# Scores of 96 attention heads: pairs of heads in one 8 MB store, with two output buffers

## The chip, the core and the metric

The kernel runs on one core of a Trainium2 chip. The metric is the time of one execution on the device, in microseconds (us). Before the change it is 1062.99 us, the median of three runs (1062.89 to 1064.05).

The engines that matter here: TensorE (PE in the profile) multiplies, its weight loads have a row of their own (PEld), VectorE (DVE) and ScalarE (ACT) copy results from PSUM, TensorE's output memory, to SBUF, the working memory of 128 partitions. GpSimd (POOL) casts the inputs. SyncE (SP) issues the stores; sixteen DMA engines carry all transfers.

## What is computed

For every one of 8 x 12 = 96 heads, a matrix of 1024 x 1024 dot products of length 64:

```
q, k: float32 [8, 12, 1024, 64]
out = np.einsum('bhid,bhjd->bhij', q, k).astype(np.float32)
```

The inputs are 50 MB, the output is 403 MB: 4 MB for each head.

## The kernel before

The heads are taken in blocks of 2, 2, 4, 8, 8 and then six times 12 (`sizes`, line 33). Each block has its q and k as raw float32 (`load`, line 66), casts them to half precision on POOL (`cast_quads`, line 113, or `cast_rows`, line 90, for the first two blocks) and transposes them so that the 64 elements of a row lie along partitions: the first two blocks by TensorE (`transpose_rows`, line 147), the others by DVE (`transpose_quads`, line 139). The transposed `qT` and `kT` hold half of a block's heads in partitions 0 to 63 and the other half in partitions 64 to 127.

`scores` (line 156) then makes one head. Its 1024 output rows are split over 128 partitions, eight neighbouring rows to each. For each of these eight (index t) two products, of 512 columns each, use 128 columns of qT as weights and fill 1024 columns of a PSUM tile. From the second head on, a PSUM tile holds two t (`w = 2`: 128 x 2048, two such tiles in PSUM), and ACT copies each to the output tile `o_sb` (line 181); the first head uses smaller tiles, copied by DVE and ACT in turn (lines 179 and 181). When the head's tile is full, SP issues one store of 4 MB, in which each partition has 32 KB in one piece (line 185).

Program order is pinned on each engine. The order is written by hand: while a block is being computed, the casts of the next ones are queued on POOL (`to_half`, line 225), the transposes of the next block on DVE (the `side` work of `block`, line 238), and the loads of the block after that on ACT's queue (`LOADS`, line 263). A load waits until the casts have read the raw tile that it overwrites; a transpose waits for its cast.

The buffers: three output tiles of 32 KB a partition (`out_pool`, line 45), one of which first holds the raw inputs of the first three blocks (`early`, line 196); two raw tiles, five half precision tiles, and two each of qT and kT.

Of the kernel before, what the change touches and what calls it, by code (L numbers as in the profile page):

```python
# [9 lines left out]
F32 = mybir.dt.float32  # L10
P = 128

@with_exitstack
def kernel(
# [6 lines left out]
    nc = tc.nc  # L21

    B, H, S, D = q.shape
    NT = S // P
    BH = B * H
# [4 lines left out]
    kf = k.rearrange("b h s d -> (b h s) d")  # L30
    of = out.rearrange("b h i j -> (b h) i j")

    sizes = [2, 2, 4, 8, 8] + [12] * ((BH - 24) // 12)
    assert sum(sizes) == BH
    PE_BLOCKS = 2
    NMAX = max(sizes)
    CHUNK = 48 * 32

    consts = ctx.enter_context(tc.tile_pool(name="consts", bufs=1))
    ident = consts.tile([P, P], F16)  # L40

    in_pool = ctx.enter_context(tc.tile_pool(name="in_pool", bufs=2))
    half_pool = ctx.enter_context(tc.tile_pool(name="half_pool", bufs=5))
    tr_pool = ctx.enter_context(tc.tile_pool(name="tr_pool", bufs=2))
    out_pool = ctx.enter_context(tc.tile_pool(name="out_pool", bufs=3))

    pin = tc.keep_in_program_order

    def half_tile():
        half_sb = half_pool.tile([P, CHUNK], F16, tag="half")  # L50
        return half_sb

    class Block:
# [3 lines left out]
        def __init__(self, first, N, by_pe):  # L57
# [5 lines left out]
            self.halves = {}  # L63
            self.cut = max(1, self.R * 32 // CHUNK + (self.R * 32 % CHUNK > 0))

# [78 lines left out]
            )[:, c * m : (c + 1) * m]  # L144
            pin(nc.vector.transpose(out=dst, in_=src))  # L145

        def transpose_rows(self, x, ps_pool, copy):
            ps = ps_pool.tile([P, S], F32, tag="po")
            t_ps = ps.bitcast(F16)[:, : NT * P].rearrange("c (t m) -> c t m", m=P)
            for t in range(NT):  # L150
                pin(nc.tensor.transpose(t_ps[:, t], self.rows[x][:, t], ident))  # L151
            dst = (self.qT, self.kT)[x][:, :S].rearrange("c (m t) -> c m t", t=NT)
            src = t_ps.rearrange("c t m -> c m t")
            pin(copy(out=dst, in_=src))  # L154

        def scores(self, n, side, ps_pool, w):

            half, g = divmod(n, self.N // 2)
            cs = slice(half * D, (half + 1) * D)

            qT = self.qT.rearrange("c (g m t) -> c g t m", t=NT, m=P)
            kT = self.kT.rearrange("c (g j) -> c g j", j=S)
            o_sb = out_pool.tile([P, NT, S], F32, tag="out")
            for u in range(NT // w):
                ps = ps_pool.tile([P, w * S], F32, tag="po")
                for tt in range(w):
                    for j in range(2):
                        js = slice(j * 512, (j + 1) * 512)
                        at = tt * S + j * 512
                        pin(  # L170
                            nc.tensor.matmul(  # L171
                                ps[:, at : at + 512],
                                qT[cs, g, w * u + tt],
                                kT[cs, g, js],
                            )
                        )
                dst = o_sb[:, w * u : w * u + w].rearrange("p t j -> p (t j)")
                if w == 1 and u % 2:
                    pin(nc.vector.tensor_copy(out=dst, in_=ps))  # L179
                else:  # L180
                    pin(nc.scalar.copy(out=dst, in_=ps))  # L181
                for do in side.get(u, []):
                    do()
            pin(
                nc.sync.dma_start(
                    out=of[self.first + n].rearrange("(p t) j -> p (t j)", p=P),
                    in_=o_sb.rearrange("p t j -> p (t j)"),
                )
            )

    blocks, first = [], 0
    for i, N in enumerate(sizes):
        blocks.append(Block(first, N, i < PE_BLOCKS))
        first += N

    early = out_pool.tile([P, NT, S], F32, tag="out")
    raw = early.rearrange("p t j -> p (t j)")
    at = 0
    for b in blocks[:3]:
        for x in range(2):  # L200
# [11 lines left out]
    def next_load(eng):  # L212
        if stream:
            b, x = stream.pop(0)
            b.load(x, eng)
# [9 lines left out]
    def to_half(last):  # L225
        while casts:
            i, c = casts[0]
            if i > last or (blocks[i], c[0]) in stream:
                return
            blocks[i].cast_quads(*c)  # L230
            casts.pop(0)
# [3 lines left out]
            b.cast_rows(x)  # L235
    to_half(2)

    def block(i, heads, ps_pool, w):
        b = blocks[i]
        nxt = blocks[i + 1] if i + 1 < len(blocks) else None  # L240
        for n in heads:
            side = {}
            if nxt and nxt.by_pe:
                if n == 1:
                    side = {
                        u: [
                            lambda x=u // 2: nxt.transpose_rows(
                                x, ps_pool, nc.vector.tensor_copy
                            )
                        ]  # L250
                        for u in (1, 3)
                    }
            elif nxt:
                parts = nxt.chunks()
                some = [s for m, s in enumerate(parts) if m * b.N // len(parts) == n]
                side = {0: [lambda s=s: nxt.transpose_quads(*s) for s in some]}

            if n in LOADS.get(i, (6, 8)):
                side[1] = side.get(1, []) + [lambda: next_load(nc.scalar)]
            b.scores(n, side, ps_pool, w)  # L260
            to_half(i + 2 + (n == b.N - 1))

    LOADS = {0: (), 1: (), 2: (1, 3), 3: (4, 6), 4: (4, 6)}

    blocks[0].alloc()
    blocks[1].alloc()
    with tc.tile_pool(name="first_pool", bufs=4, space=bass.MemoryType.PSUM) as pool:
        for x in range(2):
            blocks[0].transpose_rows(x, pool, (nc.vector.tensor_copy, nc.scalar.copy)[x])
        block(0, [0], pool, 1)  # L270
    po_pool = ctx.enter_context(
        tc.tile_pool(name="po_pool", bufs=2, space=bass.MemoryType.PSUM)
    )
    block(0, [1], po_pool, 2)
    for i in range(1, len(blocks)):
        if i + 1 < len(blocks):
            blocks[i + 1].alloc()
        block(i, range(blocks[i].N), po_pool, 2)


# [28 lines left out]
```

## Time and profile before

| What | Value |
|---|---|
| Median of three runs | 1062.99 us |
| Profiled execution | 1063.03 us |
| its span, first to last instruction | 1061.2 us |
| HBM read / written | 50.33 MB / 402.65 MB, 427 GB/s over the span |
| TensorE products, line 171 | 1536 of 64 x 512, 696.9 us busy, 617 ns each |
| ACT copies, line 181 | 380 of 128 x 2048 at 1869 ns, 4 of 128 x 1024 at 1012 ns |
| DVE copies, line 179 | 4 of 128 x 1024 at 1224 ns |
| DVE transposes, line 145 | 48 of 128 x 1536, about 8.1 us; 20 of 128 x 1024, about 4.95 us |
| POOL casts, line 127 | 192 of 32 x 1536 at 1460 ns; 80 of 32 x 1024 at 1034 ns |
| Stores, line 185 | 96 of 4096 KB, 21.8 us from issue to landing (median) |

A row of the profile's groups gives line, engine, operation, the tiles written and read, count, time busy and mean duration of one. The products are pipelined, so that 617 ns is the length of one and not the distance between two. The slices cut the span into 40 equal parts; a digit is the share in tenths that an engine, or the mean of the 16 DMA engines, was busy. A wait is told as who waited, for what, how long in total, how often, and the longest. In the timeline a row merges neighbouring instructions of one kind; the bracket is the idle time before the first and what ended it.

### The profile page before, as it was taken

To read this page: it belongs to the slowest core of one execution; us is meant where nothing else is said; L and a number is where in the kernel's file an instruction comes from. 1 tells how busy PE (TensorE), PEld (TensorE's weight loads), DVE (VectorE), ACT (ScalarE), POOL (GpSimd) and SP (SyncE) were. 2 spreads that over 40 slices of the span, in tenths; PEclk is the share of its full clock that TensorE was granted. 3 is DMA by queue.
4 is the path that set the end of the run, shared out by engine and by line. 5 is a ranking of instruction groups with operands and counts; after the bars stand their busy time and mean duration, and the time that the engine had idled before them with its cause. 6 is when DMAs were issued, how large, how long until landed. Compare 5 with 4: busy or idle time off the path is not lost.

```text
span 1061.2 us, 4282 instructions
## 1 busy us (share of the span) xinstructions
PE 701.0 (66%) x1568; PEld 241.5 (23%) x1568; DVE 471.3 (44%) x75; ACT 697.3 (66%) x386; POOL 368.3 (35%) x286
## 2 busy tenths in 40 slices
PE   6866755765677557775577855777557777778770
PEld 2322211221222112221122211222112222222220
DVE  2999502990795007960079600795007950000000
ACT  4866755755677556775577755777557777777771
POOL 6967228607720463304633046320463200000000
DMA  9999999999999999999999999999999999999997
GB/s 375 434 435 434 434 432 429 432 430 429 429 434 431 429 438 429 435 422 428 434 434 433 425 424 437 432 431 426 432 430 434 434 434 430 430 435 430 433 431 319
DMA packets 17588, 453.25 MB, mean 427 GB/s; under 512 B 1952, under 2 KB 1952, under 8 KB 2976
## 3 DMA queue, kind: packets, MB, share of 16 engines
q1 hardware_dynamic: 14688, 406.85, 89.2%
q10 hardware_dynamic: 2880, 46.14, 10.3%
q8 instruction: 12, 0.20, 0.1%
q14 instruction: 8, 0.07, 0.0%
HBM read 50.33 MB, written 402.65 MB: 427 GB/s over the span
## 4 chain that ended last, share of the span: by engine, by line
DMA 71%; ACT 18%; PE 8%; issue 1%; DVE 0%; POOL 0%; ACTq 0%; SPq 0%
DMA out_dram<-o_sb 71%; ACT o_sb L181 18%; PE ps L171 8%; DMA early<-in_q_dram 0%; PE ps L151 0%; POOL half_sb L97 0%; ACTq L181 0%; DVE kT L154 0%; DVE o_sb L179 0%; ACT kT L154 0%; SPq L84 0%
## 5 line engine op out<-in xcount | busy, mean ns | idle before, releaser
L181 ACT COPY o_sb<-ps 128x2048 f32<-128x2048 f32 (+1 forms) x384 | 695.0, 1860 | 334.6 <-DMA out_dram<-o_sb 306.2
L171 PE MATMUL ps<-kT,qT 64*128 64x512 f16 x1536 | 696.9, 617 | 329.2 <-ACT o_sb L181 325.5
L127 POOL CAST half_sb<-x_sb 32x1536 f16<-32x1536 f32 (+1 forms) x256 | 346.5, 1353 | 454.5 <-DMA x_sb<-in_q_dram 315.0
L171 PEld LDWEIGHTS <-qT 64*128 64x128 f16 x1536 | 238.3, 157 | 786.0 <-issue 781.3
L145 DVE STREAM_TRANSPOSE qT<-half_sb 128x1536 f16<-128x1536 f16 (+1 forms) x34 | 232.7, 7140 | 372.0 <-issue 314.9
L145 DVE STREAM_TRANSPOSE kT<-half_sb 128x1536 f16<-128x1536 f16 (+1 forms) x34 | 234.3, 7198 | 0.0
L127 POOL CAST half_sb<-early 32x1024 f16<-32x1024 f32 x16 | 16.5, 1034 | 3.9 <-DMA early<-in_q_dram 3.2
L151 PE MATMUL ps<-ident,half_sb 128*128 128x128 f16 x32 | 4.1, 308 | 6.6 <-POOL half_sb L97 6.0
L154 DVE COPY qT<-ps 128x1024 f16<-128x1024 f16 x2 | 2.5, 1225 | 12.1 <-PE ps L151 12.1
L179 DVE COPY o_sb<-ps 128x1024 f32<-128x1024 f32 x4 | 4.9, 1224 | 4.3 <-PE ps L171 4.3
L97 POOL CAST half_sb<-early 128x512 f16<-128x512 f32 x8 | 4.6, 613 | 4.1 <-DMA early<-in_q_dram 4.1
L151 PEld LDWEIGHTS <-half_sb 128*128 128x128 f16 x32 | 3.2, 139 | 8.4 <-POOL half_sb L97 6.3
L154 ACT ACT_TABLE_LOAD x1 | 1.3, 1283 | 5.6 <-DMA early<-in_q_dram 5.6
L154 DVE COPY kT<-ps 128x1024 f16<-128x1024 f16 x1 | 1.2, 1225 | 4.3 <-PE ps L151 4.3
L154 ACT COPY kT<-ps 128x1024 f16<-128x1024 f16 x1 | 1.0, 1012 | 1.2 <-PE ps L151 1.2
masks.py:199 POOL TENSOR_SCALAR_AFFINE_SELECT ident<-ident 128x128 f16<-128x128 f16 x1 | 0.3, 292 | 0.1
masks.py:197 POOL MEMSET ident<- 128x128 f16 x1 | 0.2, 204 | 0.3 <-POOLq L293 0.3
L293 POOL MEMSET const-float32-0.0<- 128x1 f32 x1 | 0.1, 98 | 0.2 <-issue 0.2
L293 POOL MEMSET const-bfloat16-1.0<- 128x1 bf16 x1 | 0.1, 100 | 0.0
L293 POOL MEMSET const-uint8-127<- 128x1 uint8 x1 | 0.1, 100 | 0.0
L293 POOL MEMSET const-float32-1.0<- 128x1 f32 x1 | 0.1, 98 | 0.0
## 6 DMA issues: line engine op xcount, KB each, us to landing
out_dram<-o_sb SPq DMA_DIRECT2D x96, 4096.0 KB, 21.8
x_sb<-in_q_dram ACTq DMA_DIRECT2D x6, 3072.0 KB, 22.2
x_sb<-in_k_dram ACTq DMA_DIRECT2D x6, 3072.0 KB, 21.9
x_sb<-in_k_dram ACTq DMA_DIRECT2D x2, 2048.0 KB, 19.0
x_sb<-in_q_dram SPq DMA_DIRECT2D x1, 2048.0 KB, 18.2
x_sb<-in_q_dram ACTq DMA_DIRECT2D x1, 2048.0 KB, 18.5
early<-in_k_dram ACTq DMA_DIRECT2D x4, 256.0 KB, 5.0
early<-in_q_dram SPq DMA_DIRECT2D x4, 256.0 KB, 4.7
```

Of the source, the lines that this page charges most:

```text
L97: nc.gpsimd.tensor_copy(out=self.rows[x][:, :, half], in_=self.raw[x][:, half * n : (half + 1) * n].rearrange("p (r d) -> p r d", d=D),)
L127: nc.gpsimd.tensor_copy(out=half_sb[q0 : q0 + 32].rearrange("p (r d) -> p r d", d=32), in_=raw[32 * b : 32 * b + 32, c * m : (c + 1) * m, h],)
L145: pin(nc.vector.transpose(out=dst, in_=src))
L151: pin(nc.tensor.transpose(t_ps[:, t], self.rows[x][:, t], ident))
L154: pin(copy(out=dst, in_=src))
L171: nc.tensor.matmul(ps[:, at : at + 512], qT[cs, g, w * u + tt], kT[cs, g, js],)
L179: pin(nc.vector.tensor_copy(out=dst, in_=ps))
L181: pin(nc.scalar.copy(out=dst, in_=ps))
L293: nc = _bacc.Bacc("TRN2", target_bir_lowering=False, num_devices=1)
```

## The change

Blocks become 2, 2, 4 and then eleven times 8. From the third block on, `scores` makes two heads at a time. Each head's rows are now split over 64 partitions, sixteen rows to each, so that the first head of a pair fills partitions 0 to 63 of the output tile and the second head partitions 64 to 127. A product takes 64 columns of qT as weights, and four products (two heads by two column halves) fill a PSUM tile of 128 x 1024. The pair has sixteen such tiles. It ends in one store of 8 MB, in which each partition has 64 KB in one piece. The first two blocks keep products of 128 columns and a store for each head, but also use the larger output tile.

There are two output tiles of 64 KB a partition in place of three of 32 KB, and four PSUM tiles of 128 x 1024 in place of two of 128 x 2048 throughout. The copies of a pair are shared: from the fourth block on, DVE copies tiles 1, 3, 5, 7 and 9 and ACT the other eleven; ACT alone copies those of the second and third block, and those of the first block's second head. The DVE transposes of the next block are queued after tile 10 of a pair and the loads after tile 3 (after tile 12 in the third block). Loads of the smaller blocks are 2 MB each. There are seven half precision tiles, of 32 x 32 columns in place of 48 x 32.

```diff
-    sizes = [2, 2, 4, 8, 8] + [12] * ((BH - 24) // 12)
+    sizes = [2, 2, 4] + [8] * ((BH - 8) // 8)
-    CHUNK = 48 * 32
+    CHUNK = 32 * 32
-    half_pool = ctx.enter_context(tc.tile_pool(name="half_pool", bufs=5))
+    half_pool = ctx.enter_context(tc.tile_pool(name="half_pool", bufs=7))
-    out_pool = ctx.enter_context(tc.tile_pool(name="out_pool", bufs=3))
+    out_pool = ctx.enter_context(tc.tile_pool(name="out_pool", bufs=2))
+    po_pool = ctx.enter_context(
+        tc.tile_pool(name="po_pool", bufs=4, space=bass.MemoryType.PSUM)
+    )
...
-        def scores(self, n, side, ps_pool, w):
+        def scores(self, n, side, by_dve):
+            o_sb = out_pool.tile([P, 2, NT, S], F32, tag="out")
             kT = self.kT.rearrange("c (g j) -> c g j", j=S)
+            both = not self.by_pe
+            M = 64 if both else P
+            T = S // M
+            qT = self.qT.rearrange("c (g m t) -> c g t m", t=T, m=M)
+            for v in range(2 * NT):
+                ps = po_pool.tile([P, S], F32, tag="po")
+                for j in range(2):
+                    js = slice(j * 512, (j + 1) * 512)
+                    for i in range(2) if both else [0]:
+                        h, t = (n + i, v) if both else (n + v // NT, v % NT)
+                        half, g = divmod(h, self.N // 2)
+                        cs = slice(half * D, (half + 1) * D)
                         pin(
                             nc.tensor.matmul(
-                                ps[:, at : at + 512],
-                                qT[cs, g, w * u + tt],
+                                ps[i * M : (i + 1) * M, js],
+                                qT[cs, g, t],
                                 kT[cs, g, js],
                             )
                         )
+                dst = o_sb[:, v // NT, v % NT]
+                copy = nc.vector.tensor_copy if v in by_dve else nc.scalar.copy
+                pin(copy(out=dst, in_=ps))
+                for do in side.get(v, []):
+                    do()
...
+            if both:
+                dst = of[self.first + n : self.first + n + 2]
+                pin(
+                    nc.sync.dma_start(
+                        out=dst.rearrange("h (p t) j -> (h p) (t j)", p=M),
+                        in_=o_sb.rearrange("p i t j -> p (i t j)"),
+                    )
+                )
...
+        for n in range(0, b.N, 2):
...
+                side = {10: [lambda s=s: nxt.transpose_quads(*s) for s in some]}
+            if n in LOADS.get(i, (2, 4)):
+                side[12 if i == 2 else 3] = [lambda: next_load(nc.scalar)]
+            by_dve = {0: (1, 3, 5, 7), 1: (), 2: ()}.get(i, (1, 3, 5, 7, 9))
+            b.scores(n, side, by_dve)
+            to_half(i + 2 + (n == b.N - 2))
```

More of the change, by code (lines that the diff above doesn't have):

```diff
@@ L145, in transpose_quads, with transpose_rows @@
             pin(nc.vector.transpose(out=dst, in_=src))
-        def transpose_rows(self, x, ps_pool, copy):
-            ps = ps_pool.tile([P, S], F32, tag="po")
+        def transpose_rows(self, x, copy):
+            ps = po_pool.tile([P, S], F32, tag="po")
             t_ps = ps.bitcast(F16)[:, : NT * P].rearrange("c (t m) -> c t m", m=P)
@@ L154, in transpose_rows @@
             pin(copy(out=dst, in_=src))
-        def scores(self, n, side, ps_pool, w):
-            half, g = divmod(n, self.N // 2)
-            cs = slice(half * D, (half + 1) * D)
-            qT = self.qT.rearrange("c (g m t) -> c g t m", t=NT, m=P)
+        def scores(self, n, side, by_dve):
+            o_sb = out_pool.tile([P, 2, NT, S], F32, tag="out")
             kT = self.kT.rearrange("c (g j) -> c g j", j=S)
[L163 to L169, printed above, removed]
+            both = not self.by_pe
[3 more added lines that the diff above has]
+            for v in range(2 * NT):
+                ps = po_pool.tile([P, S], F32, tag="po")
+                for j in range(2):
[4 more added lines that the diff above has]
+                        cs = slice(half * D, (half + 1) * D)
                         pin(
                             nc.tensor.matmul(
-                                ps[:, at : at + 512],
-                                qT[cs, g, w * u + tt],
+                                ps[i * M : (i + 1) * M, js],
+                                qT[cs, g, t],
                                 kT[cs, g, js],
@@ L176, in scores @@
                         )
[L177 to L182, printed above, removed]
-                    do()
[L184 to L187, printed above, removed]
+                dst = o_sb[:, v // NT, v % NT]
+                copy = nc.vector.tensor_copy if v in by_dve else nc.scalar.copy
+                pin(copy(out=dst, in_=ps))
+                for do in side.get(v, []):
+                    do()
+                if not both and v % NT == NT - 1:
+                    i = v // NT
+                    pin(
+                        nc.sync.dma_start(
+                            out=of[self.first + n + i].rearrange(
+                                "(p t) j -> p (t j)", p=P
+                            ),
+                            in_=o_sb[:, i].rearrange("p t j -> p (t j)"),
+                        )
+                    )
+            if both:
+                dst = of[self.first + n : self.first + n + 2]
+                pin(
+                    nc.sync.dma_start(
+                        out=dst.rearrange("h (p t) j -> (h p) (t j)", p=M),
+                        in_=o_sb.rearrange("p i t j -> p (i t j)"),
+                    )
                 )
-            )
     blocks, first = [], 0
@@ L194 @@
         first += N
-    early = out_pool.tile([P, NT, S], F32, tag="out")
-    raw = early.rearrange("p t j -> p (t j)")
+    early = out_pool.tile([P, 2, NT, S], F32, tag="out")
+    raw = early.rearrange("p i t j -> p (i t j)")
     at = 0
@@ L236 @@
     to_half(2)
-    def block(i, heads, ps_pool, w):
-        b = blocks[i]
+    LOADS = {0: (), 1: (), 2: (0, 2)}
+    blocks[0].alloc()
+    blocks[1].alloc()
+    for x in range(2):
+        blocks[0].transpose_rows(x, (nc.vector.tensor_copy, nc.scalar.copy)[x])
+    for i, b in enumerate(blocks):
         nxt = blocks[i + 1] if i + 1 < len(blocks) else None
-        for n in heads:
+        if nxt and i:
+            nxt.alloc()
+        for n in range(0, b.N, 2):
             side = {}
             if nxt and nxt.by_pe:
[L244 to L252, printed above, removed]
+                side = {
+                    v: [lambda x=x: nxt.transpose_rows(x, nc.vector.tensor_copy)]
+                    for x, v in enumerate((10, 14))
+                }
@@ L253, in block @@
             elif nxt:
                 parts = nxt.chunks()
[L255 to L278, printed above, removed]
+                some = [
+                    s for m, s in enumerate(parts) if m * b.N // len(parts) // 2 == n // 2
+                ]
```

## The prediction

> **What bounds the kernel now.** I read the page's slices and queues first, then the waits, the timeline of two heads, and last the tail in short windows.
>
> ```profile
> DMA  9999999999999999999999999999999999999997
> GB/s 375 434 435 434 434 432 429 432 430 429 429 434 431 429 438 429 435 422 428 434 434 433 425 424 437 432 431 426 432 430 434 434 434 430 430 435 430 433 431 319
> ...
> q1 hardware_dynamic: 14688, 406.85, 89.2%
> q10 hardware_dynamic: 2880, 46.14, 10.3%
> q8 instruction: 12, 0.20, 0.1%
> ```
>
> The queues fill 99.6% of the span: the transfers are the bound, and only what shortens them, starves them or burdens one of their 16 engines moves the end.
>
> ```profile
> ACT o_sb L181 <- DMA out_dram<-o_sb: 306.2, 90, 7.2
> ```
> ```profile
> 412.46 3.63 PE L171 MATMUL ps<-kT,qT 64*128 64x512 f16 x8 [2.88 <-ACT o_sb L181]
> 412.46 0.14 PEld L171 LDWEIGHTS <-qT 64*128 64x128 f16 x1 [3.35 <-issue]
> 412.84 0.16 PEld L171 LDWEIGHTS <-qT 64*128 64x128 f16 x1 [0.24 <-issue]
> 413.27 0.16 PEld L171 LDWEIGHTS <-qT 64*128 64x128 f16 x1 [0.27 <-issue]
> 413.69 0.16 PEld L171 LDWEIGHTS <-qT 64*128 64x128 f16 x1 [0.27 <-issue]
> ```
>
> Compute waits for stores to land (306 us in 90 waits), never the reverse. The second of these gives TensorE's price: a product every 0.427 us (413.27 less 412.84, with rounding), its weights loaded in 0.16 us while the one before runs.
>
> ```profile
> 1040.00:1052.00 12.00, 0.00 (x0) 0.00 (x0) 0.00 (x0) 0.00 (x0) 0.00 (x0) 1.00 1.01 437
> 1052.00:1054.00 2.00, 0.00 (x0) 0.00 (x0) 0.00 (x0) 0.00 (x0) 0.00 (x0) 1.00 0.76 328
> 1054.00:1056.00 2.00, 0.00 (x0) 0.00 (x0) 0.00 (x0) 0.00 (x0) 0.00 (x0) 1.00 0.27 115
> 1056.00:1058.00 2.00, 0.00 (x0) 0.00 (x0) 0.00 (x0) 0.00 (x0) 0.00 (x0) 1.00 0.08 33
> 1058.00:1060.00 2.00, 0.00 (x0) 0.00 (x0) 0.00 (x0) 0.00 (x0) 0.00 (x0) 1.00 0.04 16
> ```
>
> The tail (last columns: DMA share, GB/s) shows what an average hides: one engine moves 437/16 = 27 GB/s, so from 1056 us about one is at work, and compute has long ended. **One engine is late**, 2.8 us behind the next and 6.8 behind the first (the 16 increments of the last landing). The packet records say why. Between 540 and 600 us fifteen engines take 1213 ns for each 32 KB packet (one a longer packet once), this one 1226.5 on average, in steps of about 5 and 9 ns. After 1040 us, with no compute engine running, it takes 1213 like the rest. Within 300-345, 540-600 and 860-940 us its excess goes with the instructions started during the packet (correlation 0.54 to 0.67, slope 2.0 to 2.4 ns each). Over 768 packets the excess is some 12.5 ns x 768 = 9.6 us, and 2.24 ns x 4282 instructions is 9.6 as well.
>
> **The change part by part.** The sum is against the profiled execution: 1063.03 us, span 1061.2, the 1.8 around it taken as unchanged. It is within 0.1 us of the median, 1062.99.
>
> *Store packets.* The records give 309, 611, 912 and 1213 ns for 8, 16, 24 and 32 KB: 301.3 per 8 KB and 8 on top, of which neighbours overlap 3.5. No 64 KB packet is in the trace; on this line it takes 2418, against 2 x 1213. Eight packets an engine for each of 46 pairs (92 of 96 heads; the first four keep 4 MB stores) save 8 x 5 ns and one 5.5 ns completion: 46 x 45 ns = **-2.1 us**. Bounds: 0 (the chip cuts it into 32 KB again) and -3.4 (all 8 ns, and 9 for the completion).
>
> The Trainium skill, "DMA: Bandwidth & Descriptors", section "Anatomy of one DMA", gives a transfer about 2.0 us fixed beside bytes/436 GB/s: 46 transfers fewer would be up to 92 us if they queued one behind the other. Here buffers come round every 9.77 us for 4 MiB (ACT's restarts at 1001.95, 1011.72, 1021.49), which is 429 GB/s; the fixed part is hidden, and the row decides.
>
> *Loads.* Blocks of eight load 16 KB a partition: 22 transfers of 8 x 611 ns instead of 4 of those and 12 of 8 x 912. With overlap and completions that is **+0.3**.
>
> *Instruction fetch.* TensorE's 3136 instructions come in 12 fetches of 16 KB, 0.93 us each on one engine. The change doubles products (64 a pair, 3008 with the first blocks, against 1536) and their weight loads: 6080 with the transposes, 24 fetches. Twelve more over 16 engines: **+0.8** (0 to 1.9).
>
> *TensorE.* A product of 64 columns streams the same 512 columns, so a pair has 64 x 0.427 = 27.3 us of streams where two heads had 13.7. They fit only if the two heads' products, on different halves of the columns, run together. No row shows such a pair. Bounds: 0.427 us for two, or 0.854. I take 0.43: the halves share neither weights nor PSUM partitions, and the weight loads above already run under products on the same rows.
>
> A rule speaks against it: the Trainium skill, "TensorE: Matmul & The Clock Gate", section "Part 3", says weights load under a running matmul only when the row group differs, and here both heads have the same. The rows above contradict that for one tile. By the rule two products would cost 0.43 + 0.16, still hidden by the sum below. The same section gives 2.38 times for three column tiles.
>
> *The cycle with two buffers.* From a landing: PSUM holds four tiles ready; the first copy takes 1.01 (ACT's 128x1024 row, DVE's is 1.22); then TensorE makes twelve more at 4 x 0.427 / 2 = 0.86, so the last copy ends at about 1.0 + 10.3 + 1.3, and ACT's row v10 to v15 pushes it to 13.3. From a store's issue to its first packet I allow 2 us, the nearest rows being 1.0 (a load at 0.73, packet at 1.74) and 5.4 behind a backlog (store 17.54, packet 22.94). Together 15.3. The other buffer's store needs 2 x 9.68 = 19.3, so 4 us stay hidden, more under loads. DVE's two transposes of the cycle, 4.95 each, follow its fifth copy and end near 17, before the next landing. ACT now has its load queued after v3 or v12; it waits there for the casts of the block before, which POOL (8 x 1.03 a pair) ends a pair earlier.
>
> *Start.* The first two blocks keep their stores. The early buffer comes free at 30.5 as before (last cast of it), four heads' copies end at 46.8, then block 2's pair has sixteen 1.01 copies on ACT alone: issue at 63.4, first packet about 65. The 25.2 MB before it are out by 61.3 (the records reach 25.36 MB at 61.6). The load behind v12, issued at 60.3, fills all but some **+0.7** (0 to 4).
>
> *The late engine.* Instructions: +2944 on TensorE, +384 copies, +96 casts, +24 transposes, -40 transfers: +3408. At the lower slope, 2.0 ns: **+6.8**. Bounds: 0, if what burdens it goes by time, to +9.0, if by TensorE's instructions alone (9.6 x 2944/3136); below nothing is a rival. It stays fed, with the 4 us above, so all of this reaches the end.
>
> Sum: -2.1 + 0.3 + 0.8 + 0.7 + 6.8 = +6.5: **1069.5 us**. Its own range is 1065 (a lag of 5, by 1.5 ns an instruction, -3.4 and +0.3, nothing else) to 1076 (0 + 0.3 + 1.9 + 2 + 9).
>
> **Rivals.**
> - *The lag doesn't grow* (0.20). Then -0.3: 1062.7, 1061 to 1065 with the start. For it: correlations of 0.6 leave much open. Against: nothing extra once instructions end.
> - *The lag goes by packets, and halves* (0.15): 9.6/2 = 4.8 less, 1057.9, 1056 to 1061. This one ends **faster**. It decides once the lag shrinks by 1.8 us, which is where the sum passes 1060.9. For it: the excess is seen only packet by packet, 4.7 ns a step. Against: the plain packets after 1040 us.
> - *The column halves don't run together* (0.09). Then 46 x 27.3 = 1257, after some 47 us of start and before some 22 for the last copy and store: **1326**. It begins to show from 1.2 us a tile, where 5.0 + 12 x 1.2 passes 19.3; alone it would be 1.7. For it: no row shows two products at once. Against: nothing in the rows that both would need.
> - *Two buffers starve the queue* (0.06). Each us by which the 15.3 exceeds 19.3 costs up to 46; a start of 4 with the forecast's lag, or 1 us in each cycle: 1073 to 1116. For it: the reserve shrinks, since a store now lands 21.8 us after its issue (section 6) of which its own packets take 9.7, and 4 us are left after. Against: copies of 13.3 would have to grow by a third.
>
> **How the numbers follow.** The forecast has 0.50. The range, 1059 to 1076, takes in it, the unchanged lag, part of the halved one and the nearer end of starvation; outside are 0.09 for 1326, 0.04 for starvation and 0.06 for the lowest times. Within 0.2% (1060.9 to 1065.1) is about what a measurement of this kernel can tell from no change: faster 0.17 (0.15 and the low end of the unchanged lag), same 0.18, slower 0.65.
>
> **What would show it.** Packets right: 64 KB records near 2418 ns, section 3 with some 6600 fewer on q1. TensorE right: eight products of two tiles in about 1.9 us, not 3.6; wrong: TensorE busy in all slices, DMA at 8 tenths. Cycle right: ACT restarts on a landing about every 19.5 us and copies for 13, with no DMA slice under 9. Late engine right: a tail that runs longer at under 30 GB/s, and steady 64 KB packets on one engine 40 ns or more above the others. The forecast fails if that engine's excess is as before, or if the first 65 us leave the DMA idle.

## The result, and the profile after

The changed kernel takes 1079.09 us (median of four runs, 1076.74 to 1080.41) against 1063.52 us before on the same chip: 1.0145 times the time, 95% interval 1.0133 to 1.0158. The forecast was 1069.5 us in a range of 1059 to 1076. The direction was right, the size was not: the loss is 15.6 us and not 6.5, and the time lies outside the range. The profiled execution after is the fastest of the four: 1076.74 us, span 1075.0.

The page of the kernel after, its DMA slices, its rates and its queues (packets, MB, share of 16 engines):

```profile
DMA  9999999999999999999999999999999999999997
GB/s 390 429 429 437 432 433 432 413 405 431 434 407 442 428 399 430 433 425 424 430 410 411 441 430 393 421 444 420 423 427 410 412 443 398 430 456 430 427 429 337
...
q1 hardware_dynamic: 8064, 406.85, 88.4%
q10 hardware_dynamic: 3744, 46.14, 10.7%
q8 instruction: 24, 0.39, 0.1%
```

The queues are as full as before, so compute has not become the bound. What differs is in the second line: between its first and its last slice the kernel before never moved less than 422 GB/s; here ten of these slices lie between 393 and 413. Bytes are as before, q1 has 6624 packets fewer, as forecast, and the fetches (q8) are the 24 that were forecast. In q10 the loads take 10.7% of 16 engines' time where before they took 10.3.

The waits of the kernel after (who waits, for what: us in total, times, longest):

```profile
ACT o_sb L188 <- DMA out_dram<-o_sb: 362.2, 45, 10.7
PE ps L180 <- ACT o_sb L188: 340.7, 47, 10.4
DVE o_sb L188 <- DMA out_dram<-o_sb: 228.1, 43, 11.6
```

Compute still waits for stores: 45 times for ACT, once for each pair, half as often as before and longer each time.

The timeline of the kernel after, one pair near its end (start, length, engine, line, operation, count):

```profile
414.11 8.81 PE L180 MATMUL ps<-kT,qT 64*64 64x512 f16 x40 [1.32 <-DVE o_sb L188]
414.12 8.28 PEld L180 LDWEIGHTS <-qT 64*64 64x64 f16 x40 [1.85 <-issue]
```

Forty products, each of 512 streamed columns, take 8.81 us: 0.44 us for two. The two heads' products run together on the two halves of the columns, and their weights load meanwhile.

The tail of the kernel after in windows (the last two columns: DMA share, GB/s):

```profile
1068.00:1070.00 2.00, 0.00 (x0) 0.00 (x0) 0.00 (x0) 0.00 (x0) 0.00 (x0) 1.00 0.46 197
1070.00:1072.00 2.00, 0.00 (x0) 0.00 (x0) 0.00 (x0) 0.00 (x0) 0.00 (x0) 1.00 0.23 98
1072.00:1074.00 2.00, 0.00 (x0) 0.00 (x0) 0.00 (x0) 0.00 (x0) 0.00 (x0) 1.00 0.00 0
```

There is no longer one engine alone at the end: the first and the last of the 16 increments of the last landing are 4.7 us apart, 6.8 before. The forecast expected this tail to grow. (A packet counts in the window in which it starts, so the last 64 KB packets leave the last row empty.)

The packet records give 2418 ns for the typical 64 KB packet, as forecast. Without loads, over the last four stores (landings at 1016.0, 1035.3, 1054.7, 1074.0), a pair takes 19.3 us, less than two stores of before (9.77 each). The loss is therefore made earlier. Blocks show where. From the landing of one block's last store to that of the next, the nine blocks that run beside loads take 89.52 us on average, the last two 77.3.

### The profile page after: what moved, and what is told of

Its sections match the earlier page's. It is cut to its first block, busy times and chain, and to the rows that moved or that the text cites. A ratio compares the mean times of both kernels' runs of the same rounds, so it can differ in the third digit from the quotient of the medians.

```text
span 1075.0 us, 7734 instructions
## 1 busy us (share of the span) xinstructions
PE 666.5 (62%) x3040; PEld 467.8 (44%) x3040; DVE 700.7 (65%) x319; ACT 522.6 (49%) x546; POOL 385.6 (36%) x382
## 3 DMA queue, kind: packets, MB, share of 16 engines
q10 hardware_dynamic: 3744, 46.14, 10.7%
## 4 chain that ended last, share of the span: by engine, by line
DMA 64%; ACT 16%; PE 13%; DVE 2%; POOL 2%; issue 1%; ACTq 0%; POOLq 0%
DMA out_dram<-o_sb 63%; ACT o_sb L188 16%; PE ps L180 13%; DVE o_sb L188 2%; POOL half_sb L130 2%; DMA early<-in_q_dram 1%; ACTq L310 0%; ACTq L188 0%; ACTq L76 0%; POOLq L130 0%
## 5 line engine op out<-in xcount | busy, mean ns | idle before, releaser
L180 PE MATMUL ps<-kT,qT 64*64 64x512 f16 (+1 forms) x3008 | 662.7, 629 | 374.2 <-ACT o_sb L188 340.7
L188 ACT COPY o_sb<-ps 128x1024 f32<-128x1024 f32 x544 | 520.3, 1038 | 518.7 <-DMA out_dram<-o_sb 362.2
L180 PEld LDWEIGHTS <-qT 64*64 64x64 f16 (+1 forms) x3008 | 464.7, 211 | 570.2 <-issue 464.1
L130 POOL CAST half_sb<-x_sb 32x1024 f16<-32x1024 f32 x352 | 363.8, 1033 | 522.6 <-DMA x_sb<-in_q_dram 202.7
L188 DVE COPY o_sb<-ps 128x1024 f32<-128x1024 f32 x224 | 270.2, 1223 | 330.0 <-DMA out_dram<-o_sb 228.1
L148 DVE STREAM_TRANSPOSE kT<-half_sb 128x1024 f16<-128x1024 f16 x46 | 215.9, 4914 | 0.0
L148 DVE STREAM_TRANSPOSE qT<-half_sb 128x1024 f16<-128x1024 f16 x46 | 215.4, 4882 | 0.0
```

Of the source, the lines that this page charges most:

```text
L130: nc.gpsimd.tensor_copy(out=half_sb[q0 : q0 + 32].rearrange("p (r d) -> p r d", d=32), in_=raw[32 * b : 32 * b + 32, c * m : (c + 1) * m, h],)
L180: nc.tensor.matmul(ps[i * M : (i + 1) * M, js], qT[cs, g, t], kT[cs, g, js],)
L188: pin(copy(out=dst, in_=ps))
```

## The experiments

When they began there were three theories. The first is the forecast's: doubled instructions burden one DMA engine. The second: with two large buffers and 8 MB released at once, engines that finish a store early stand dry until the next one is issued. The third: the loads collide with the large stores. Each run is given with its median, and with the ratio to the kernel before on the same chip and its interval.

### e1: only the instructions, doubled in the kernel before

```diff
-                    for j in range(2):
-                        js = slice(j * 512, (j + 1) * 512)
+                    for j in range(4):
+                        js = slice(j * 256, (j + 1) * 256)
```

> The kernel before with each product cut in two of 256 columns: TensorE's instructions double (3136 to 6208), its streaming time, stores, loads and buffers stay. Theory A (one DMA engine is late in step with the instructions, TensorE's above all): 6.9 us more by 2.24 ns an instruction, up to 9.4 by TensorE's share alone, so 1070 to 1073, with that engine's 32 KB packets near 1240 ns where they were 1226. Theory B (two large output buffers let engines run dry, instructions cost nothing): no change, 1063 to 1064. Both theories at once: as A.

Measured: 1069.26 us, 1.0057 [1.0045, 1.0070]. Streams, stores and buffers are those of before; 3072 more instructions cost 6.1 us, 2.0 ns each. The tail of e1 in windows:

```profile
1054.00:1056.00 2.00, 0.00 (x0) 0.00 (x0) 0.00 (x0) 0.00 (x0) 0.00 (x0) 1.00 0.76 328
1056.00:1058.00 2.00, 0.00 (x0) 0.00 (x0) 0.00 (x0) 0.00 (x0) 0.00 (x0) 1.00 0.23 98
1058.00:1060.00 2.00, 0.00 (x0) 0.00 (x0) 0.00 (x0) 0.00 (x0) 0.00 (x0) 1.00 0.11 49
1060.00:1062.00 2.00, 0.00 (x0) 0.00 (x0) 0.00 (x0) 0.00 (x0) 0.00 (x0) 1.00 0.04 16
1062.00:1064.00 2.00, 0.00 (x0) 0.00 (x0) 0.00 (x0) 0.00 (x0) 0.00 (x0) 1.00 0.08 33
1064.00:1066.00 2.00, 0.00 (x0) 0.00 (x0) 0.00 (x0) 0.00 (x0) 0.00 (x0) 1.00 0.04 16
```

At 27 GB/s an engine, between two and four engines' worth moves from 1056 to 1060 us and about one from then on: the last landing's increments are 10.6 us apart, against 6.8 before. The first theory holds for e1. Of the 15.6 us it leaves some 9 open.

### e2, e3 and e4: the two halves of the change apart

e2 keeps the large tiles and the 8 MB store but makes each head with products of 128 columns, so that a partition has a 32 KB piece of each head:

```diff
-            both = not self.by_pe
+            both, pair = False, not self.by_pe
...
-                        out=dst.rearrange("h (p t) j -> (h p) (t j)", p=M),
-                        in_=o_sb.rearrange("p i t j -> p (i t j)"),
+                        out=dst.rearrange("i (p t) j -> p i (t j)", p=P),
+                        in_=o_sb.rearrange("p i t j -> p i (t j)"),
```

> The kernel after with 128-column products, the two heads of a pair one after the other, and still one 8 MB store for the pair, now in pieces of 32 KB: TensorE's instructions fall back to 3136, two large buffers and all the rest stay, the packets give back 2.1 us. Theory A: 1079 less 6.6 to 9.4 plus 2.1, so 1072 to 1075. Theory B: 1079 plus 2, so 1080 to 1082. If the time falls below 1068, neither.

e3 keeps the products of 64 columns but has four tiles of 32 KB, each with its own 4 MB store:

```diff
-    out_pool = ctx.enter_context(tc.tile_pool(name="out_pool", bufs=2))
+    out_pool = ctx.enter_context(tc.tile_pool(name="out_pool", bufs=4))
...
+                if v % NT == 0:
+                    o_sb = out_pool.tile([P, NT, S], F32, tag="out")
...
+                if both and v % NT == NT - 1:
+                    dst = of[self.first + n : self.first + n + 2]
+                    dst = dst.rearrange("h (p w t) j -> w (h p) (t j)", p=M, w=2)
```

> The kernel after with 64-column products, but four output tiles of 32 KB a partition and two 4 MB stores for a pair in place of two tiles of 64 KB and one store: instructions as after, stores as small and as deep as before. Theory A alone: 1079 plus the 2.1 of the packets, 1079 to 1082. Theory B alone: about as before, 1063 to 1066. Both, A with 9 us and B with the rest: 1072 to 1075, and engines no longer dry in mid run.

e4 has the four tiles of e3 and the products of e2.

> The kernel after with both undone: 128-column products, a head at a time, four tiles of 32 KB, a 4 MB store for each head. What is left of the change is blocks of eight, four small PSUM tiles and DVE's share of the copies. Theories A and B, alone or together: 1062 to 1066. Above 1068 the rest of the change costs something that neither names.

Measured: e2 1069.65 us, 1.0061 [1.0048, 1.0073]; e3 1072.04 us, 1.0086 [1.0072, 1.0100]; e4 1067.33 us, 1.0043 [1.0031, 1.0056]. So with small tiles the doubled instructions cost 4.7 us (e3 less e4). The large tiles cost 2.3 with 32 KB packets (e2 less e4) but 7.0 with 64 KB packets (after less e3). And e4, which has neither half, is still 4.2 us above before: the smaller blocks, the smaller PSUM tiles, or DVE's share of the copies.

### e5: the loads later

```diff
-                side[12 if i == 2 else 3] = [lambda: next_load(nc.scalar)]
+                side[15] = [lambda: next_load(nc.scalar)]
```

> The kernel after with its loads queued after a pair's last copy, just as the pair's store is issued, where they were queued after tile 3, so that load packets always lie beside store packets. Theory A (the late engine pays for instructions, and that is all): no change, 1078 to 1080. Theory C (with two buffers most engines run dry of stores once or twice a block, start again together, and then take their load packets in a burst that is slower than 611 ns a packet): some 4 to 8 us less, 1071 to 1075, and load packets near 611 ns. If the time rises, the loads now come too late for the casts.

Measured: 1079.12 us, 1.0147 [1.0133, 1.0161], as the kernel after. Queuing the loads twelve tiles later makes no difference to the time. The third theory in the form "the load is issued at a bad moment" fell here; that the collision is one of packets was not yet seen.

### e6 and e7: the same tiles, stored in two halves

e6 stores the first half of a pair's tile when it is full:

```diff
-            if both:
+                if both and v % NT == NT - 1:
+                    dst = of[self.first + n : self.first + n + 2]
+                    dst = dst.rearrange("h (p w t) j -> w (h p) (t j)", p=M, w=2)
...
+                            out=dst[v // NT],
+                            in_=o_sb[:, v // NT].rearrange("p t j -> p (t j)"),
```

> The kernel after with a pair's tile stored in two halves of 4 MB, the first as soon as its eight tiles are copied; still two buffers of 64 KB, now packets of 32 KB. Theory A: 1079 plus 2.1 for the packets, 1080 to 1082. Theory C: the queue gets work some 6 us earlier in each cycle, no engine is dry, so about as with four buffers, 1071 to 1074. If it stays at 1078 or more with no engine dry, the cost lies in the release of the buffers and not in the late issue.

e7 puts both halves' stores at the end of the pair in the program:

```diff
+                dst = dst.rearrange("h (p w t) j -> w (h p) (t j)", p=M, w=2)
+                for w in range(2):
...
+                            out=dst[w],
+                            in_=o_sb[:, w].rearrange("p t j -> p (t j)"),
```

> The kernel after with two stores of 4 MB in place of one of 8 MB, both issued at the end of the pair: only the packets differ, 32 KB for 64 KB. Theories A and C: 2.1 us more, 1080 to 1083. If the long packets themselves do harm (a load packet waits behind 2.4 us of store packet in place of 1.2), it is less than 1079 instead, by as much as 5.

Measured: e6 1071.14 us, 1.0074 [1.0062, 1.0087]; e7 1070.79 us, 1.0070 [1.0057, 1.0084]. Both get some 8 us back, with two large tiles. But e7 did not separate what it was meant to: SP waits only for the copies that fill a half, so the first half was still issued 6.9 us or more before the second, and each half was released by itself. Both runs change three things at once: packets of 32 KB, an earlier issue, a release by halves.

### e8: only the blocks of eight, in the kernel before

```diff
-    sizes = [2, 2, 4, 8, 8] + [12] * ((BH - 24) // 12)
+    sizes = [2, 2, 4] + [8] * ((BH - 8) // 8)
-    CHUNK = 48 * 32
+    CHUNK = 32 * 32
-    half_pool = ctx.enter_context(tc.tile_pool(name="half_pool", bufs=5))
+    half_pool = ctx.enter_context(tc.tile_pool(name="half_pool", bufs=7))
-            if n in LOADS.get(i, (6, 8)):
+            if n in LOADS.get(i, (4, 6)):
```

> The kernel before with the blocks of the kernel after (2, 2, 4, eleven times 8), casts of 32 x 1024 and seven half precision tiles; 128-column products, three buffers, copies of 128 x 2048 by ACT stay. It asks what of the 4.2 us that 128 columns and four buffers left over is due to blocks of eight. Theory A gives 120 more instructions 0.3 us and the loads 0.3: 1063.5 to 1064.5. If smaller loads, more of them and in other places, cost by themselves: 1066 to 1068.

Measured: 1066.16 us (11 runs, 1064.07 to 1068.77), 1.0029 [1.0019, 1.0040]. The blocks of eight, with the smaller casts and loads that go with them, cost some 3 us by themselves.

### e9: one 8 MB store, but packets of 32 KB

Eight floats between the halves of the tile break each partition's 64 KB in two; issue and release stay as in the kernel after.

```diff
-            o_sb = out_pool.tile([P, 2, NT, S], F32, tag="out")
+            o_sb = out_pool.tile([P, 2, NT * S + 8], F32, tag="out")
...
-                        out=dst.rearrange("h (p t) j -> (h p) (t j)", p=M),
-                        in_=o_sb.rearrange("p i t j -> p (i t j)"),
+                        out=dst.rearrange("h (p w t) j -> (h p) w (t j)", p=M, w=2),
+                        in_=o_sb[:, :, : NT * S],
```

> The kernel after, with eight floats of padding between the two 32 KB halves of the output tile: still one 8 MB store for a pair, issued once and released once, but each partition now leaves in two packets of 32 KB. It separates two things that the earlier runs changed together. If it is the coarse issue and release (one event for 8 MB, engines that are early stand dry until the next store), the time stays with the kernel after, plus the 2.1 us that the 64 KB packets saved: 1079 to 1083. If it is the 64 KB packet itself (it holds an engine for 2.4 us while loads wait behind it), the time falls to that of the split stores: 1070 to 1073.

Measured: 1072.55 us (six runs, 1069.49 to 1077.30), 1.0095 [1.0076, 1.0115]. Its runs spread more than the others', and two of the six (1076.91 and 1077.30) are as long as the fastest of the kernel after; but its interval and that of the kernel after (1.0133 to 1.0158) do not meet. Its median is the time of e3, which has four buffers and a store for each 4 MB. So with packets of 32 KB, issuing and releasing 8 MB at a time costs nothing that these runs show: **by itself the second theory falls, and the 64 KB packet is what this part of the loss needs**. Whether 64 KB packets would also cost without the coarse issue, with another store always queued, no run shows. Where they act is seen in the loads. The DMA issues of the kernel after, from its page (KB each, median us from issue to landing):

```profile
x_sb<-in_k_dram ACTq DMA_DIRECT2D x11, 2048.0 KB, 30.7
x_sb<-in_q_dram ACTq DMA_DIRECT2D x10, 2048.0 KB, 30.4
```

The same rows of e9:

```profile
x_sb<-in_k_dram ACTq DMA_DIRECT2D x11, 2048.0 KB, 20.8
x_sb<-in_q_dram ACTq DMA_DIRECT2D x10, 2048.0 KB, 21.8
```

A load of the same size needs 9 to 10 us longer beside 64 KB packets. The records say how. While loads run, about as many store packets as load packets start: 229 to 249 for the 256 load packets of a block in the kernel after, 112 to 157 for each 128 in e9. While both have work, the two queues take turns, packet by packet. A load has eight 16 KB packets on each engine, so it needs eight turns: 8 x (0.611 + 2.418) = 24.2 us beside 64 KB packets, 8 x (0.611 + 1.213) = 14.6 us beside 32 KB ones. The records agree: the 256 packets of a block's two loads form one stretch of 47 to 49 us in the kernel after, and two of 14 to 17 us each in e9.

The slow turns add no byte. What the records show beside them is a bunch of long load packets: of the 2544 after the first 60 us, 193 take over 730 ns in the kernel after (up to 2.8 us, 0.61 is the norm), 10 in e9. In most blocks some 20 come together within 2 to 6 us during the first load, for example 18 from 219.8 to 224.2 us. Their excess over 611 ns is 5.7 us for each of the 16 engines in the kernel after and 0.3 in e9.

Most of them come where an engine has no store packet left. Eight turns beside 64 KB packets take 24.2 us, but an engine's share of a whole 8 MB store is eight packets, 19.3 us. A load that starts within a store can use it up, and the engine then only reads until packets of the next store reach it. In the kernel after about 530 of the 2544 load packets begin just as another load packet ends, and 105 of these are long, with 37 of the 66 that begin after an idle moment; of some 1800 that begin as a store packet ends, 43 are. In e9 about 30 begin as a load packet ends, and none of these is long. So the second theory's dry engines do play a part, together with the slow turns.

That the long load packets are the whole price isn't shown. In e5 317 are long, with an excess of 9.2 us for each engine, at the same time as the kernel after; its store packets of 64 KB have less excess over 2418 ns, 7.4 us against 10.6. And excess as such is not time: the store packets of e9 have 11.0 us of it over 1213 ns, those of e3 5.6, and both kernels take some 1072 us.

### e10 and e11: without most loads

In both the loads of the blocks from the seventh on are left out (heads 32 to 95), and the casts read the sixth block's inputs again; e10 is otherwise the kernel after, e11 is e8.

```diff
-            b.load(x, eng)
+            if b in blocks[6:]:
+                b.raw[x] = blocks[5].raw[x]
+            else:
+                b.load(x, eng)
```

> The kernel after, with the loads of the blocks from the seventh on left out (heads 32 to 95): the casts read the sixth block's inputs again. Everything else runs as before, so the time is read only beside e11, which leaves out the same loads. If the harm of the large tiles and stores comes about only when loads mix with stores, this run is above e11 by the doubled instructions alone, less what the packets save: 4.7 to 6.1 minus 2.1, so 2.5 to 4 us. If the harm needs no loads, it is above e11 by what the full kernels show, 1079 less 1066: 11 to 14 us.

> The kernel before in blocks of eight heads (as in e8), with the loads of the blocks from the seventh on left out (heads 32 to 95), as in e10. The loads left out are 33.6 MB, at 433 GB/s some 77 us of the queues, so about 1066 less 77: 986 to 991. It is the yardstick of e10; if loads are what makes blocks of eight cost 3 us, it falls by 2 us more than the bytes.

Measured: e10 995.18 us (994.54 to 996.10), e11 985.97 us (985.70 to 987.15): 9.2 us apart, between the two expectations; a third of the heads still has its loads. Blocks separate it. Over seven blocks without loads, the third to the ninth of eight heads, e10 takes 79.02 us for each and e11 78.42: 0.60 apart. The forecast's instructions less the packets' saving are (6.8 - 2.1)/11 = 0.43 for a block. With loads, nine blocks of the kernel after take 89.52 and of e8 88.38: 1.14 apart. So half of the loss in a block needs the loads.

e10 also shows the late engine plainly. Its stores land 19.70 to 19.75 us apart for most of the run from 314 us on (one of 20.29), while 8 x 2418 ns are 19.34: the engine that lands last takes about 49 ns more for each 64 KB packet, where before it took 13.5 for each 32 KB packet. The first engine lands 5.8 us earlier. Some of the early ones then stand dry: in every such pair fewer than 16 packets are at work for a while, some 4 us of engine time in all. It doesn't lengthen the pair. And e11 ends 80.2 us before e8, where the bytes left out are worth 77.5 (33.55 MB at 433 GB/s). That hints that most of what blocks of eight cost goes with their loads; it isn't shown, since no run leaves the loads out of the kernel before.

### e12 and e13: 64 KB packets only where no loads are, and only where they are

Both take the kernel of e9 with the padding in half of the pairs: e12 in the pairs at heads 0 and 2 of a block, whose stores meet the block's loads, e13 in those at heads 4 and 6.

```diff
+            W = NT * S
+            at = W + (8 if both and n in (0, 2) else 0)
...
+                lo = v // NT * at + v % NT * S
+                dst = o_sb[:, lo : lo + S]
```

> The padding of e9 only in the pairs that begin at heads 0 and 2 of a block, whose stores are on the queues together with the block's loads; the pairs at heads 4 and 6 keep packets of 64 KB. If the harm of the 64 KB packets is done where loads take turns with them (in the kernel after some 20 load packets at a block's first load take 0.7 to 2 us each in place of 0.61), it goes away here: fewer than 40 of the 2544 load packets above 730 ns, where the kernel after has 193 and e9 has 10; loads land in 21 to 23 us and not in 30; time 1070 to 1073. If it comes from 64 KB packets wherever they are, half of the 6.5 us stays: 1075 to 1077.

> The counterpart of e12: the padding only in the pairs that begin at heads 4 and 6 of a block, whose stores meet few loads; the pairs at heads 0 and 2 keep packets of 64 KB. If the harm is done where loads take turns with 64 KB packets, it stays: some 150 to 200 load packets above 730 ns, loads landing in about 30 us, 1077 to 1081. If it comes from 64 KB packets wherever they are, half of it goes: 1075 to 1077.

Measured: e12 1070.49 us, 1.0079 [1.0066, 1.0093]; e13 1079.48 us, 1.0152 [1.0139, 1.0165]. The 64 KB packets of the pairs that meet loads do the harm, and those of the other pairs none that shows. Both kernels have the same padded tile and 7734 instructions, so the padding itself is not what helps. The DMA issues of e12:

```profile
x_sb<-in_k_dram ACTq DMA_DIRECT2D x11, 2048.0 KB, 20.7
x_sb<-in_q_dram ACTq DMA_DIRECT2D x10, 2048.0 KB, 22.2
```

And of e13:

```profile
x_sb<-in_k_dram ACTq DMA_DIRECT2D x11, 2048.0 KB, 28.5
x_sb<-in_q_dram ACTq DMA_DIRECT2D x10, 2048.0 KB, 30.6
```

Load packets over 730 ns: 11 in e12, 204 in e13 (excess 0.3 and 5.9 us for each engine). Load packets that begin just as another load packet ends: 35 in e12, 546 in e13. Blocks with loads take 88.63 us in e12 and 89.93 in e13. The rates over the slices of e13 (GB/s):

```profile
GB/s 386 430 429 438 421 422 431 431 399 428 431 411 421 438 404 419 432 424 407 418 436 397 432 421 412 422 434 424 430 401 438 398 421 422 435 424 433 446 417 349
```

The dips below 410 are there as in the kernel after.

## Why the prediction was wrong, and where it was right

- **Store packets, -2.1: this is the step that failed.** The 64 KB packet takes the 2418 ns that the step gave it, and in the last two blocks, without loads, a pair lands every 19.3 us, which is what eight such packets take; that this is the saving of 2.1 us no run shows by itself, as the last two blocks of e2, with 32 KB packets, are as short (77.4 and 77.8 us). But the step counted a packet's own time only. Beside loads it takes turns with them, a load needs eight turns of 3.0 us, engines run out of store packets meanwhile, and in most blocks some 20 load packets come out long. (The section that this step cites for 2.0 us fixed a transfer describes DMAs issued by GpSimd; these stores are issued by SP, and the step rightly went by the row of 9.77 us.) By medians, the kernel after less e9, the change from 32 to 64 KB packets costs 6.5 us (by the ratios 0.50% of 1063, 5.3 us, give or take some 2.5), where -2.1 was forecast. On the profiled executions it adds up: nine blocks with loads 0.60 us longer each than in e9 (5.4), 1.6 up to the first of these blocks, and 2.8 less in the last two, where the late engine is no longer the last; together 4.3, the difference of the spans (1075.0 and 1070.7).
- **Loads, +0.3: too small.** Blocks of eight alone cost 3.0 us (e8). Between the records of before and e8 the excess of packets over their usual time grows by 2.9 us for each engine on the stores and falls by 1.2 on the loads. Why store packets lengthen with more and smaller loads is open. e4 says that the rest of the change without both of its halves costs about 1 us more (1067.33 less 1066.16), within their spread.
- **The late engine, +6.8: right in its cause, somewhat large.** 6.1 in e1, 4.7 between e3 and e4. (The copies are 380 more and not 384, which is worth nothing here.) Of the bounds, 0 is excluded. Both rivals that stood on this engine fall: the lag grows, and it doesn't go by packets, since e10 with half as many has an excess per byte 1.8 times that of before (49 ns for 64 KB against 13.5 for 32 KB), as its instructions are (7686 against 4282). Only its sign in the profile failed: the tail shrank, because with two buffers an early engine can't run further ahead than the next store, so that the lag shows in the distance of the landings and not at the end.
- **TensorE: right.** 0.44 us for two products, forecast 0.43, and not the 0.59 that the prediction worked out from the page's rule on row groups: the weights load under the products of the same rows. The case of 1326 us falls.
- **The cycle with two buffers: right.** From a landing to the next issue 13.07 us (forecast 13.3), 15.4 in the pairs with a load, where TensorE waits twice for a copy of DVE. The engine that lands last always had 4 us of packets left: the next landing came 6.2 us or more after the issue, less the 2 allowed to the first packet. The rival of starvation names a time that the kernel reached (1073 to 1116), but not by its path: early engines do run dry, and e9, with the same issue and release, loses nothing by it against e3, nor e10 without loads. What neither the rival nor the forecast had is that an engine dry of stores may still have packets of a load to read.
- **Instruction fetch, +0.8:** 24 fetches as forecast; not tried alone, and part of e1's 6.1. (Twelve of 0.93 us over 16 engines are 0.7.)
- **Start, +0.7:** 1.9 us by the landing of the first eight heads (113.7 us against 111.8 in e8), of which the padding of e9 takes 1.6 away: the first two 8 MB stores meet loads too.

By medians the 15.9 us to the 1063.2 of before on the experiments' chips are: blocks of eight 3.0, the rest of e4 1.2, instructions 4.7, large tiles with 32 KB packets 0.5 (e9 less e3), 64 KB packets 6.5. The chain of differences holds the order in which they were taken; e2 shows that parts interact (large tiles cost 2.3 there).

The Trainium skill, "DMA: Bandwidth & Descriptors", section "Queues, rings and completion order", has the rule that the prediction left out: an engine goes round the queues that have work, and changes queue only at the end of a packet. The runs agree with the turns, and differ in their size: the page has a packet of typically 9 to 17 descriptors drained before a turn ends. If a piece in the records is one such descriptor, which no run shows, the eight pieces of a load would go in one turn, by estimate 8 x 0.611 = 4.9 us on an engine; here every piece of 16, 32 or 64 KB was a turn of its own while both queues had work.

What stays open is why load packets become long when engines read several in a row. Many engines reading at once is not enough: in e9 250 load packets begin with 13 to 16 engines reading, none over 730 ns; in the kernel after 67 of 211 such packets are longer.

No version here beats the kernel before; e7, the best with the new products and large tiles, stays at 1.0070.

## What to carry to other kernels

Price a larger DMA packet by what it makes the other queue wait, not by its own time: count the pieces of the load on one engine, and multiply by the sum of one piece from each queue. Compare that with the work that the store queue holds: here it was 24.2 us against 19.3. If a large piece pays, use it where no other queue has work, as e12 did (its gain over e9 is within their noise), and break it with a few bytes of padding elsewhere. On a kernel whose DMA queues are full, doubling the instruction count isn't free even where TensorE has time: here it was 2 ns for each.

## What was not expected of the hardware

- Two queues on one engine share it by turns of one recorded packet, at both sizes tried: 229 to 249 store packets of 64 KB to 256 load packets of 16 KB, and 112 to 157 of 32 KB to 128.
- A skew between DMA engines of 5.8 us, with early ones dry in each pair, does not lengthen a pair where no loads run (e10): the engine that lands last sets the pace.
- Eight floats of padding in a tile's row set the packet size, and with it 6.5 us, without another instruction: both kernels have 7734.
